# A normalised input transposed by channel tile, with the gain applied on the way out of PSUM

## The chip, the cores and the metric

The kernel runs on one core of one Trainium2 chip. The metric is the device time of one execution in microseconds (us), as the median of several runs. TensorE is called PE in the profile, its weight loads PEld, VectorE DVE, ScalarE ACT, GpSimd POOL and SyncE SP (it issues the DMAs here). Each engine works through its own instructions in order and waits on semaphores for the others.

## The reference, cut to what matters

One layer with two parallel groups of heads (differential attention and a gated recurrence) and a feed-forward block with a convolution. 16 meta tokens stand ahead of 1024 tokens of width 1024. The part concerned is the first normalisation and the first projection:

```python
def rmsnorm(x, g):
    xf = x.astype(jnp.float32)
    y = xf * lax.rsqrt(jnp.mean(xf * xf, axis=-1, keepdims=True) + EPS)
    return (y * g.astype(jnp.float32)).astype(x.dtype)

h = jnp.concatenate([meta, x], axis=1)      # 1040 x 1024
a = rmsnorm(h, ln_mix_pre[l])
proj = a @ w_in[l]                          # 1024 x 3584
```

Attention, the recurrence, the output projection and the feed-forward block follow; the change doesn't touch them.

## The kernel before, in words

Tokens are cut into nine blocks: block 0 has the 16 meta tokens, blocks 1 to 8 have 128 tokens each. Three blocks make a token group, of 272, 384 and 384 tokens (`GROUPS`). The 1024 channels are cut into eight channel tiles of 128.

The projection needs the normalised input with channels on the partitions. It is kept in two parts: `ahi`, the value rounded to the matmul's format, and `alo`, what the rounding left (each 8 tiles by 1040 tokens). Weights are split in the same way into `hi` and `lo`. A product of one channel tile is three matmuls (hi by ahi, hi by alo, lo by ahi; `proj_step`, L218), so one projection of 128 columns for one token group is 24 matmuls into one PSUM bank. They are called products below. Head 0 of the attention is projected first: queries (`dq`), keys (`dk`) and values (`dv`), each for three token groups: 3 x 3 x 24 = 216 products. After it comes head 0's recurrence input (`hf`, the first dense projection), with attention beside it.

Before the change, a block is made ready like this. `pre_stat` (L244): ScalarE squares the block with an accumulator for the row sums, then a logarithm and an exponential give the reciprocal root (`rstd_of`, L157). `pre_scale` (L252): VectorE multiplies block, root and gain in two passes of 512 columns; the gain `gb` lies on all 128 partitions, made at the start by a matmul of a row of ones with the gain row (L793 to L797). `pre_turn` (L257): TensorE transposes four channel tiles of the block into one PSUM bank. `pre_hi` and `pre_lo` (L265, L268): ScalarE copies the bank to `ahi`, VectorE subtracts that from the bank into `alo`, 512 columns each.

The order of TensorE's instructions is that of the program (`manual_schedule`). On the other engines a scheduler orders the instructions, except while `state["ordered"]` is set: then VectorE and ScalarE keep program order, too. `interleave` (L59) decides where side work stands between products: it takes products worth `lead` ns first, then alternately one step of the side work and products worth `fill` ns. Blocks 0 to 2 are made ready by a sequence written out by hand (L789 to L827); `head0_first` (L829) gives the 48 query and key products and the 24 value products of the first token group; blocks 3 to 5 stand among its value products, one half block at a time (L887), and blocks 6 to 8 among head 0's products of the second group (L890). Small constants (`smalls`) and the tables of the relative bias (`bias_tables`, four matmuls) follow. The loads are all on SP's queue: gain, blocks 0 to 2, weights, blocks 3 to 8, then small constants and the next weights.

`pools`: PSUM has three kinds of tiles of two buffers each: `ip` (one bank, for products), `m` (one bank) and `S` (two banks). VectorE's subtraction for the weights' `lo` part stands on GpSimd (`split`, L144; L871 for the value weights).

Of the kernel before, what the change touches and what calls it, by code (L numbers as in the profile page):

```python
# [17 lines left out]
P = 128  # L18
META = 16
# [17 lines left out]
def start(i):  # L37
    return 0 if i == 0 else META + P * (i - 1)
# [20 lines left out]
def interleave(dense, sides, fill, lead=0):  # L59
    sides = list(sides)  # L60
    live = True

    def feed(budget):
        nonlocal live
        while live and budget > 0:
            c = next(dense, False)
            if c is False:
                live = False
            elif c is None:
                return  # L70
# [11 lines left out]
    feed(1e12)  # L82


@with_exitstack
def layer_kernel(ctx: ExitStack, tc: tile.TileContext, x, meta, table, lbl, gpre, gpost, win,
# [54 lines left out]
    def ps_s(name):  # L141
        return pp.tile([P, 2, 512], F32, tag="S", name=name)
# [88 lines left out]
    gb = zp.tile([P, D], F32, tag="gb", name="gb", bufs=1)  # L231
    ones = zp.tile([P, 384], F32, tag="rb", name="ones", bufs=1)[:1, :P]
    G.memset(ones, 1.0)

    xts, xss = {}, {}
# [8 lines left out]
    def pre_stat(i):  # L244
        r = rows(i)
        xss[i] = zp.tile([P, D], F32, tag="xs", name=f"xs{i}", bufs=3)
        ss = zp.tile([P, 1], F32, tag="ss", name=f"ss{i}", bufs=3)
        A.activation(xss[i][:r], xts[i][:r], AF.Square, accum_out=ss[:r])
        rstd_of(ss[:r], ss[:r], D)
        return ss  # L250

    def pre_scale(i, half, ss):  # L252
        r = rows(i)
        cs = slice(512 * half, 512 * half + 512)
        V.scalar_tensor_tensor(xss[i][:r, cs], xts[i][:r, cs], ss[:r], gb[:r, cs], ALU.mult, ALU.mult)

    def pre_turn(i, half, pt):  # L257
        r = rows(i)
        for j in range(4):
            k = 4 * half + j  # L260
            T.transpose(pt[:, j * r:(j + 1) * r], xss[i][:r, P * k: P * (k + 1)], ident[:r, :r])
        pv = pt[:, : 4 * r].rearrange("p (k t) -> p k t", k=4)
        return pv, slice(4 * half, 4 * half + 4), slice(start(i), start(i) + r)

    def pre_hi(pv, ks, s):  # L265
        return A.copy(ahi[:, ks, s], pv)

    def pre_lo(pv, ks, s):  # L268
        return V.tensor_tensor(alo[:, ks, s], pv, ahi[:, ks, s].bitcast(F32), op=ALU.subtract)

    def pre_block(i):
        with tc.issue_after(last_hi.ins):
            ss = pre_stat(i)
        for half in range(2):
            pre_scale(i, half, ss)
        pt = ps_s(f"px{i}")
        for half in range(2):
            out_ = pre_turn(i, half, pt[:, half])
            pre_hi(*out_)
            pre_lo(*out_)  # L280
            yield
# [473 lines left out]
    grow = zp.tile([P, D], F32, tag="xt", name="grow", bufs=3)[:1]  # L755
    SY.dma_start(grow, gpre)
# [4 lines left out]

    def raw_tile(j, c):
        if 2 * j + c < 3 or (j, c) == (1, 0):
            return wp.tile([P, 512], F32, tag="wr", name=f"wr_{tiles[j][1]}_{c}", bufs=3)
        n = 2 * j + c - 3
        return spare[0][:, 512 * n: 512 * (n + 1)]

    raws, parts = {}, [[None, None] for _ in range(3)]

    def load_raw(j, c):  # L770
        raws[j, c] = raw_tile(j, c)
        SY.dma_start(raws[j, c], win[tiles[j][0]][:, 512 * c: 512 * (c + 1)])
# [8 lines left out]
    load_x(5, spare[2][:, D:2 * D])  # L781

    def weights(j, c):
        hi = wp.tile([P, 512], F32R, tag="wh", name=f"wh_{tiles[j][1]}_{c}", bufs=4)
        lo = wp.tile([P, 512], F32R, tag="wl", name=f"wl_{tiles[j][1]}_{c}", bufs=4)
        split(hi, lo, raws[j, c])
        parts[j][c] = hi, lo

    state["ordered"] = True  # L789
    stat = {}  # L790
    for i in range(3):
        stat[i] = pre_stat(i)
    for half in range(2):  # L793
        cs = slice(512 * half, 512 * half + 512)
        pt = ps_m(f"pg{half}")
        T.matmul(pt, ones, grow[:, cs], start=True, stop=True)
        V.tensor_copy(gb[:, cs], pt)  # L797
        if half == 0:
            pre_scale(0, 0, stat[0])
    load_x(6)  # L800
    banks0 = {0: [ps_m(f"px0_{half}") for half in range(2)]}
    for i in (1, 2):
        both = ps_s(f"px{i}")
        banks0[i] = [both[:, half] for half in range(2)]
    turned = {}

    def turn(i, half):
        turned[i, half] = pre_turn(i, half, banks0[i][half])

    for i in (1, 2):  # L810
        for half in range(2):
            pre_scale(i, half, stat[i])
    pre_scale(0, 1, stat[0])
    for i, half in ((0, 0), (1, 0), (1, 1), (2, 0), (2, 1)):
        turn(i, half)
    pre_hi(*turned[0, 0])
    pre_hi(*turned[1, 0])
    weights(0, 0)
    pre_hi(*turned[2, 0])
    for i in range(3):  # L820
        pre_lo(*turned[i, 0])
    weights(1, 0)
    pre_hi(*turned[1, 1])
    weights(0, 1)
    last_hi = pre_hi(*turned[2, 1])
    weights(1, 1)
    load_x(7)  # L827

    def head0_first():  # L829
# [15 lines left out]
        yield from part(0, 0, 1, ahi)  # L845
        yield from part(0, 0, 0, alo)
        yield from part(1, 0, 0, alo)
        yield from part(1, 0, 1, ahi)
# [10 lines left out]
    first_group = head0_first()  # L859
    for _ in range(6):  # L860
        next(first_group)
    turn(0, 1)
    pre_hi(*turned[0, 1])
    for i in range(3):
        last_lo = pre_lo(*turned[i, 1])
    state["ordered"] = False
    third = [ap_.tile([P, 4, 512], F32R, tag="pb", name=f"w3{c}", bufs=2) for c in range(2)]
    for c in range(2):
        with tc.issue_after(last_lo.ins):
            V.tensor_copy(third[c][:, 0], raws[2, c])  # L870
            G.tensor_tensor(third[c][:, 1], raws[2, c], third[c][:, 0].bitcast(F32), op=ALU.subtract)  # L871
        parts[2][c] = third[c][:, 0], third[c][:, 1]

# [7 lines left out]
    def pre_blocks(bs):  # L881
        for i in bs:
            yield from pre_block(i)
            if i == 3:
                load_x(8)

    interleave(first_group, [pre_blocks([3, 4, 5])], 450, 4900)  # L887
    with tc.issue_after(last_lo.ins):
        smalls()
    interleave(head0(1), [pre_blocks([6, 7, 8])], 1800, 1800)  # L890
    interleave(head0(2), [bias_tables()], 2600)
# [630 lines left out]
def _arrays(inputs):  # L1522
    import numpy as np

    def c(a):
        return np.ascontiguousarray(a)
# [10 lines left out]
    for lv in range(5):  # L1537
# [8 lines left out]
        "gpre": c(i["ln_mix_pre"]),  # L1546
# [34 lines left out]
```

## Time and profile before

| what | us |
|---|---|
| median of 3 runs | 1350.29 |
| lowest and highest run | 1346.78, 1351.36 |
| the profiled execution's own time | 1337.81 |
| its span, first to last instruction | 1335.9 |

All durations are from the one profiled execution. In a row of the timeline stand start, duration, engine, line, operation, output<-input, shape and count; in brackets the idle time of the engine before it, and what ended it. In a row of groups stand busy time and the mean duration of one in ns, then the idle time before the group. In a row of windows stand the stretch, then busy time and count of PE, PEld, DVE, ACT and POOL, the granted clock of TensorE as a share of full speed, the DMA engines' share and GB/s. L53 is the helper through which all instructions of VectorE and ScalarE are issued; tiles tell them apart: `xs` the scaled block, `px` a transposed one in PSUM, `pi_dq`, `pi_dk` and `pi_dv` products in PSUM, `ss` sums and roots, `w` the value weights.

### The profile page before, as it was taken

Reading aid. Unit: us, or ns where it says so; the run is one execution under the profiler, and the core shown is the slowest. Engines: PE = TensorE matmul, PEld = TensorE weight load, DVE = VectorE, ACT = ScalarE, POOL = GpSimd, SP = SyncE. Lnnn points to the kernel's source line nnn. Section 1 sums busy time; section 2 is a strip of 40 time slices with the busy share of each in tenths; the row PEclk is TensorE's granted clock in tenths of the full one; section 3 lists DMA queues with packets and bytes.
Section 4 is the critical chain, followed back from the end, with each engine's and each line's share of the span. In section 5 each row is a group of like instructions: output and inputs, shape, how many; then the busy total and the mean of one; then the engine's idle time right before and its main releaser. Section 6 shows DMA issues by size and latency. Waiting matters only on the chain.

```text
span 1335.9 us, 26155 instructions
## 1 busy us (share of the span) xinstructions
PE 1288.3 (96%) x10172; PEld 1187.0 (89%) x10172; DVE 909.4 (68%) x1534; ACT 692.6 (52%) x1633; POOL 426.3 (32%) x334
## 2 busy tenths in 40 slices
PE   7999999999999998999999999999999999999997
PEld 6899989989999998677889999999999998888875
DVE  7565647574746474637798777787787776697586
ACT  7465356535654665237674454444445444454453
POOL 3211212021212110325035666656666640010121
PEclk8999999999999999999999999999999999999999
DMA  5242334143311223657512222223222226955263
GB/s 208 101 141 72 116 119 144 62 140 126 120 48 53 80 88 123 199 182 261 196 48 88 88 91 76 72 92 107 77 90 72 73 95 197 335 185 166 87 205 118
DMA packets 99426, 165.00 MB, mean 124 GB/s; under 512 B 10035, under 2 KB 34899, under 8 KB 99302
## 3 DMA queue, kind: packets, MB, share of 16 engines
q1 hardware_dynamic: 99302, 163.32, 37.2%
q8 instruction: 80, 1.31, 0.4%
q14 instruction: 44, 0.36, 0.1%
HBM read 122.65 MB, written 40.63 MB: 122 GB/s over the span
## 4 chain that ended last, share of the span: by engine, by line
PE 47%; DVE 5%; ACT 3%; issue 3%; DMA 2%; POOL 2%; SPq 0%; DVEq 0%; POOLq 0%; ACTq 0%
PE pd L1427 5%; PE pd L1428 5%; PE pd L1426 5%; PE pb L1268 4%; PE pb L1270 4%; PE pb L1269 4%; PE pc L1268 2%; PE pc L1269 2%; PE pa L1268 2%; PE pa L1270 2%; PE pc L1270 2%; PE pa L1269 2%; PE py L948 1%; PE py L944 1%; PE py L946 1%
## 5 line engine op out<-in xcount | busy, mean ns | idle before, releaser
L1268 PE MATMUL pb<-t,uh 128*128 128x258 f32 x504 | 142.8, 283 | 4.5 <-DVE u L53 4.5
L1269 PE MATMUL pb<-t,uh 128*128 128x258 f32 x504 | 141.7, 281 | 0.0
L1270 PE MATMUL pb<-t,ul 128*128 128x258 f32 x504 | 141.6, 281 | 0.0
L1427 PE MATMUL pd<-wl,gh 128*128 128x512 f32 x308 | 121.9, 396 | 0.1
L1426 PE MATMUL pd<-wh,gh 128*128 128x512 f32 x308 | 121.7, 395 | 0.0
L1428 PE MATMUL pd<-wh,gl 128*128 128x512 f32 x308 | 121.7, 395 | 0.0
L53 DVE SCALAR_TENSOR_TENSOR c<-uu,cwt,c 128x514 f32<-128x514 f32 (+1 forms) x88 | 95.9, 1090 | 20.6 <-ACT c L53 19.9
L1235 POOL TENSOR_TENSOR c<-c,c 128x514 f32<-128x514 f32 (+1 forms) x44 | 63.4, 1440 | 124.7 <-ACT c L53 122.7
L1268 PEld LDWEIGHTS pb<-t,uh 128*128 128x128 f32 x504 | 95.4, 189 | 5.9 <-DVE u L53 5.5
L1269 PEld LDWEIGHTS pb<-t,uh 128*128 128x128 f32 x504 | 95.5, 189 | 0.0
L1270 PEld LDWEIGHTS pb<-t,ul 128*128 128x128 f32 x504 | 95.2, 189 | 0.0
L1268 PE MATMUL pa<-t,uh 128*128 128x258 f32 (+1 forms) x336 | 95.2, 283 | 0.0
L1270 PE MATMUL pa<-t,ul 128*128 128x258 f32 (+1 forms) x336 | 95.0, 283 | 0.0
L1269 PE MATMUL pa<-t,uh 128*128 128x258 f32 (+1 forms) x336 | 94.8, 282 | 0.0
L1268 PE MATMUL pc<-t,uh 128*128 128x258 f32 (+1 forms) x336 | 94.4, 281 | 0.0
L1269 PE MATMUL pc<-t,uh 128*128 128x258 f32 (+1 forms) x336 | 94.0, 280 | 0.0
L1270 PE MATMUL pc<-t,ul 128*128 128x258 f32 (+1 forms) x336 | 93.7, 279 | 0.0
L53 DVE SCALAR_TENSOR_TENSOR c<-ug,cwt,c 128x514 f32<-128x514 f32 (+1 forms) x88 | 84.6, 962 | 2.7 <-ACT c L53 2.0
L147 POOL TENSOR_TENSOR ul<-ws,uh 128x512 fp32r<-128x512 f32 x42 | 60.7, 1445 | 39.4 <-ACT uh L53 34.1
L1427 PEld LDWEIGHTS pd<-wl,gh 128*128 128x128 f32 x308 | 57.7, 187 | 14.9 <-DVE wl L53 0.9
L1426 PEld LDWEIGHTS pd<-wh,gh 128*128 128x128 f32 x308 | 57.7, 187 | 14.1
L1428 PEld LDWEIGHTS pd<-wh,gl 128*128 128x128 f32 x308 | 57.7, 187 | 14.1
(364 smaller groups left out, 4122.0 us busy)
## 6 DMA issues: line engine op xcount, KB each, us to landing
ra<-in_wup_dram SPq DMA_DIRECT2D x88, 256.0 KB, 2.9
mp<-msc SPq DMA_DIRECT2D x23, 512.0 KB, 5.8
wd<-in_wdown_dram SPq DMA_DIRECT2D x44, 256.0 KB, 4.6
tsc<-wd SPq DMA_DIRECT2D x44, 256.0 KB, 3.1
wi<-tsc SPq DMA_DIRECT2D x44, 256.0 KB, 2.8
gi<-gsc SPq DMA_DIRECT2D x33, 256.0 KB, 4.0
wi<-in_wdown_dram SPq DMA_DIRECT2D x33, 256.0 KB, 2.8
gsc<-c SPq DMA_DIRECT2D x22, 257.0 KB, 2.1
```

The costliest lines, as they stand in the source:

```text
L53: ins = call(*args, **kw)
L147: (eng or G).tensor_tensor(lo, raw, hi.bitcast(F32), op=ALU.subtract)
L944: T.matmul(py[:r], mh, hi, start=(first and k == ks[0]), stop=False)
L946: T.matmul(py[:r], mh, lo, start=False, stop=False)
L948: T.matmul(py[:r], ml, hi, start=False, stop=(last and k == ks[-1]))
L1235: G.tensor_tensor(cg, cg, cu, op=ALU.mult)
L1268: T.matmul(pt, hi[:, s], th[:, k], start=(first and k == 0), stop=False, skip_group_check=True)
L1269: T.matmul(pt, hi[:, s], tl[:, k], start=False, stop=False, skip_group_check=True)
L1270: T.matmul(pt, lo[:, s], th[:, k], start=False, stop=(k == 3), skip_group_check=True)
L1426: T.matmul(py, gh[:, s], wh, start=(k == 0 and pr not in (3, 7)), stop=False, skip_group_check=True)
L1427: T.matmul(py, gh[:, s], wl, start=False, stop=False, skip_group_check=True)
L1428: T.matmul(py, gl[:, s], wh, start=False, stop=(k == NH - 1), skip_group_check=True)
```

## The change

Gain, scaling, transposes and copies are arranged by channel tile over the three blocks of a group, instead of by block.

- The gain arrives as a column per channel tile (`gt`, 128 x 8). It is applied when a transposed tile leaves PSUM: ScalarE multiplies by the tile's column into `ahi`, VectorE multiplies and subtracts into `alo` in one instruction. The matmul and the copies that spread the gain go.
- Scaling multiplies a block by its root alone, in place.
- For each channel tile, the transposes of the group's three blocks go side by side into one PSUM bank; one copy and one subtraction of 272 or 384 columns follow. Products can start on a channel tile when that tile is out.
- Squares of blocks 2 (half) and 3 move to VectorE. Roots of blocks 3 to 5 and of 6 to 8 are taken together, after the last square of each three.
- 40 dummy transposes of the identity stand among the first ones.
- The whole of head 0 is one stream of products (`chain_all`), and one stream of side work runs beside it: group 1's tiles, small constants, group 2's tiles, the bias tables. Blocks 7 and 8 are loaded behind the others into the buffers of blocks 0 and 1.

The core of the diff:

```diff
-    def pre_stat(i):
-        A.activation(xss[i][:r], xts[i][:r], AF.Square, accum_out=ss[:r])
-        rstd_of(ss[:r], ss[:r], D)
-    def pre_scale(i, half, ss):
-        V.scalar_tensor_tensor(xss[i][:r, cs], xts[i][:r, cs], ss[:r], gb[:r, cs], ALU.mult, ALU.mult)
...
+    def sq_a(i, cols=slice(0, D)):
+        r = rows(i)
+        return A.activation(junk_a[:r, cols], xts[i][:r, cols], AF.Square, accum_out=ssq[:r, i:i + 1])
+
+    def sq_v(i, cols=slice(0, D), to=None):
+        r, to = rows(i), i if to is None else to
+        return V.scalar_tensor_tensor(junk_v[:r, cols], xts[i][:r, cols], 1.0, xts[i][:r, cols],
+                                      ALU.mult, ALU.mult, accum_out=ssq[:r, to:to + 1])
+
+    def scale(i, cols=slice(0, D)):
+        r = rows(i)
+        V.tensor_scalar(xts[i][:r, cols], xts[i][:r, cols], ssq[:r, i:i + 1], None, ALU.mult)
+
+    def turn(i, k, pt, t0):
+        r = rows(i)
+        o = start(i) - t0
+        T.transpose(pt[:, o:o + r], xts[i][:r, P * k: P * (k + 1)], ident[:r, :r])
+
+    def halves_in(k, pt, t0, t1):
+        s = slice(t0, t1)
+        hi = A.mul(ahi[:, k, s], pt[:, : t1 - t0], gt[:, k:k + 1])
+        return hi, V.scalar_tensor_tensor(alo[:, k, s], pt[:, : t1 - t0], gt[:, k:k + 1], ahi[:, k, s].bitcast(F32), ALU.mult, ALU.subtract)
...
+    def pre_group(g):
+        b0, b1 = GROUPS[g]
+        t0, t1 = start(b0), start(b1 - 1) + P
+        if g > 1:
+            with tc.issue_after(last_hl[0].ins):
+                for i in range(b0, b1):
+                    sq_a(i)
+            rstd_of(ssq[:, b0:b1], ssq[:, b0:b1], D)
+        for i in range(b0, b1):
+            scale(i)
+        banks = px_banks(g)
+        for k in range(KD):
+            pt = next(banks)
+            for i in range(b0, b1):
+                turn(i, k, pt, t0)
+            last_hl[:] = halves_in(k, pt, t0, t1)
+            yield 1 if g < 2 else 2.4
...
+    sq_a(0)
+    rstd_of(ssq[:META, 0:1], ssq[:META, 0:1], D)
+    sq_a(1)
+    rstd_of(ssq[:, 1:2], ssq[:, 1:2], D)
+    sq_a(2, slice(0, 512))
+    scale(0)
+    sq_v(2, slice(512, D), NBLK)
+    V.tensor_tensor(ssq[:, 2:3], ssq[:, 2:3], ssq[:, NBLK:NBLK + 1], op=ALU.add)
+    scale(1)
+    weights(0, 0, V.tensor_copy)
+    rstd_of(ssq[:, 2:3], ssq[:, 2:3], D)
+    for half in range(2):
+        scale(2, slice(512 * half, 512 * half + 512))
+    idle_turns(24)
...
+    for k in range(KD):
+        if k > 3:
+            pxs.append(next(banks0))
+            for i in range(2):
+                turn(i, k, pxs[k], t0)
+        turn(2, k, pxs[k], t0)
+        halves_in(k, pxs[k], t0, t1)
+        if k == 0:
+            weights(1, 0, V.tensor_copy)
+        if k == 3:
+            weights(0, 1, A.copy)
+        if k == 5:
+            weights(1, 1, A.copy)
+        advance((0, 1, 1, 6, 4, 4, 4, 4)[k])
+    for c in range(2):
+        weights(2, c, V.tensor_copy)
+    sq_v(3)
+    sq_a(4)
+    sq_a(5)
+    rstd_of(ssq[:, 3:6], ssq[:, 3:6], D)
+    state["ordered"] = False
+    load_x(7)
+    load_x(8)
+
+    def sides():
+        yield from pre_group(1)
...
+        yield from pre_group(2)
...
-    interleave(first_group, [pre_blocks([3, 4, 5])], 450, 4900)
-    interleave(head0(1), [pre_blocks([6, 7, 8])], 1800, 1800)
-    interleave(head0(2), [bias_tables()], 2600)
+    interleave(chain_all(first_group, head0(1), head0(2)), [sides()], 460, 2300)
```

More of the change, by code (lines that the diff above doesn't have):

```diff
@@ L82, in interleave, with chain_all @@
     feed(1e12)
+def chain_all(*its):
+    for it in its:
+        yield from it
 @with_exitstack
@@ L258, in pre_turn @@
+    def turn(i, k, pt, t0):
         r = rows(i)
[L259 to L269, printed above, removed]
@@ new lines, in px_banks @@
+    def px_banks(g):
+        b = []
+        for k in (0, 2):
+            both = ps_s(f"px{g}_{k}")
+            b += [both[:, 0], both[:, 1]]
+        yield from b
+        yield ps_m(f"px{g}_4")
+        yield ps_m(f"px{g}_5")
+        both = ps_s(f"px{g}_6")
+        yield both[:, 0]
+        yield both[:, 1]
+    last_hl = []
+    def pre_group(g):
[15 more added lines that the diff above has]
+            yield 1 if g < 2 else 2.4
@@ L781, in layer_kernel, with weights @@
     load_x(5, spare[2][:, D:2 * D])
[L783 to L786, printed above, removed]
-        parts[j][c] = hi, lo
[L789 to L827, printed above, removed]
+    load_x(6)
+    def weights(j, c, copy):
+        if j < 2:
+            hi = wp.tile([P, 512], F32R, tag="wh", name=f"wh_{tiles[j][1]}_{c}", bufs=4)
+            lo = wp.tile([P, 512], F32R, tag="wl", name=f"wl_{tiles[j][1]}_{c}", bufs=4)
+        else:
+            both = ap_.tile([P, 4, 512], F32R, tag="pb", name=f"w3{c}", bufs=2)
+            hi, lo = both[:, 0], both[:, 1]
+        copy(hi, raws[j, c])
+        G.tensor_tensor(lo, raws[j, c], hi.bitcast(F32), op=ALU.subtract)
+        parts[j][c] = hi, lo
     def head0_first():
@@ L857, in head0_first @@
             yield from proj_step(pts[2], parts[2], k, t0, t1, lambda: tiles[2][2](0, *g0, t0, t1, pts[2]))
[L859 to L872, printed above, removed]
     def head0(g):
@@ new lines, in layer_kernel, with idle_turns @@
+    pxs = [next(banks0) for _ in range(4)]
+    warm = ps_m("warm")
+    def idle_turns(n):
+        for _ in range(n):
+            T.transpose(warm[:, :P], ident, ident)
+    state["ordered"] = True
+    sq_a(0)
[8 more added lines that the diff above has]
+    weights(0, 0, V.tensor_copy)
```

74 lines of the change are left out of this document (37 added, 37 removed).

## The prediction

> **What bounds the kernel now.** I read the page first: the busy shares, and the row of the granted clock in 40 slices of 33.4 us.
>
> ```profile
> PE 1288.3 (96%) x10172; PEld 1187.0 (89%) x10172; DVE 909.4 (68%) x1534; ACT 692.6 (52%) x1633; POOL 426.3 (32%) x334
> PEclk8999999999999999999999999999999999999999
> ```
>
> TensorE is busy for 96% of the span, so time that TensorE loses early is not won back later. Only the first slice shows a lower clock, and the change lies there. So next come the windows of 10 us, with the granted clock behind the busy times.
>
> ```profile
> 10.00:20.00 10.00, 9.32 (x69) 8.61 (x67) 7.13 (x12) 8.78 (x21) 8.17 (x6) 1.00 0.99 370
> 20.00:30.00 10.00, 5.92 (x27) 5.50 (x27) 8.96 (x19) 6.01 (x16) 0.00 (x0) 0.61 0.25 80
> 30.00:40.00 10.00, 9.51 (x59) 9.08 (x59) 7.79 (x22) 6.79 (x18) 0.00 (x0) 0.88 0.01 2
> 40.00:50.00 10.00, 10.00 (x61) 9.15 (x60) 4.30 (x8) 4.65 (x9) 0.00 (x0) 1.00 0.01 2
> ```
>
> The stretch from 20 to 32 us is what can be won: TensorE is busy for 5.92 of 10 us, at a clock of 0.61. The timeline shows both losses.
>
> ```profile
> 12.17 0.77 PE L837 MATMUL pi_dq<-ahi,wh_dq 128*128 128x272 f32 x4 [0.68 <-ACT ahi L53]
> ...
> 19.69 0.29 PE L222 MATMUL pi_dv<-ahi,w 128*128 128x272 f32 x1
> ...
> 19.81 0.29 PE L224 MATMUL pi_dv<-alo,w 128*128 128x272 f32 x1
> ...
> 23.38 1.11 PE L261 MATMUL px<-ident,xs 128*128 128x128 f32 x4 [3.28 <-DVE alo L53]
> ...
> 26.28 0.43 PE L224 MATMUL pi_dv<-alo,w 128*128 128x272 f32 x1
> 26.51 0.43 PE L226 MATMUL pi_dv<-ahi,w 128*128 128x272 f32 x1
> ...
> 27.96 1.12 PE L261 MATMUL px<-ident,xs 128*128 128x128 f32 x4 [0.80 <-DVE alo L53]
> ...
> 32.94 0.29 PE L224 MATMUL pi_dv<-alo,w 128*128 128x272 f32 x1
> 33.06 0.29 PE L226 MATMUL pi_dv<-ahi,w 128*128 128x272 f32 x1
> ...
> 33.19 0.34 PE L222 MATMUL pi_dq<-ahi,wh_dq 128*128 128x384 f32 x1
> 33.37 0.34 PE L224 MATMUL pi_dq<-alo,wh_dq 128*128 128x384 f32 x1
> ...
> 65.65 0.34 PE L226 MATMUL pi_dv<-ahi,w 128*128 128x384 f32 x1
> ```
>
> Products of 272 columns start 0.12 us apart at 19.7 us. After an idle stretch of 3.28 us they start 0.23 us apart (26.28 to 26.51), and 0.12 apart again at 32.94: the half clock held from 23.4 to about 32.2, that is 8.9 us, with two more gaps in it; from the end of the 0.80 us gap at 27.96 to the return it was 4.3 us. The second token group's products begin at 33.19 (call that point T), and head 0 ends at 66.0.
>
> **The change part by part.** Everything after head 0 keeps its instructions, so I ask when T comes and what lies between T and the end of head 0.
>
> *Start, to the first group's products.* The row matmul of the gain (two 128x512 outputs), two copies of it and the gain in the scaling go; the gain is a per-partition scalar in the instructions that leave PSUM. Block 2's square is shared by two engines. What stays is a chain: squares of blocks 1 and 2, the root, scaling, transposes, copies.
>
> ```profile
> 5.27 1.06 ACT L53 ACTIVATE xs<-xt 128x1024 f32<-128x1024 f32 x1 [0.35 <-DMA xt<-in_x_dram]
> 8.38 0.20 ACT L53 ACTIVATE ss<-ss 128x1 f32<-128x1 f32 x1
> L53 ACT ACTIVATE xs<-X_in 128x1024 f32<-128x1024 f32 x4 | 4.2, 1057 | 0.0
> L53 ACT ACTIVATION_READ_ACCUMULATOR xs<-X_in 128x1 f32 x4 | 0.8, 193 | 0.0
> L53 ACT ACTIVATE ss<-ss,eps 128x1 f32<-128x1 f32 x8 | 2.4, 296 | 0.1
> L53 DVE TENSOR_SCALAR rb<-rb 128x256 f32<-128x256 f32 x4 | 1.5, 366 | 0.1
> L53 DVE TENSOR_SCALAR kr<-kr 128x272 f32<-128x272 f32 x4 | 1.2, 294 | 0.0
> L53 DVE CAST w<-X_in 128x512 fp32r<-128x512 f32 x2 | 1.0, 538 | 0.0
> L53 ACT ACTIVATE kr<-pi_hf 128x272 f32<-128x272 f32 x4 | 1.6, 398 | 1.0 <-PE pi_hf L226 1.0
> ```
>
> Block 2's root ends at 8.6 as before: half a square fewer on ScalarE (0.5 us), but a VectorE addition and a wait for it instead. A scaling reads one tensor and one scalar per partition. The shapes nearest to it take 0.37 us for 256 and 0.29 us for 272 columns. At that slope plus a fixed 0.2, 1024 columns cost 0.75 us and 512 0.48. Without that rate it would be 1.28 us (the row further down). I take 0.75, since both rows are of its form. VectorE does block 1's scaling, one weight cast, then block 2's first half: done at 9.6, and the first copy out of PSUM at 10.05. Each copy covers 272 columns (0.40 us on ScalarE). From channel tile 4 on, TensorE puts four products (0.5 us) between two tiles' transposes and the copies follow it, two weight casts of 0.62 us between them: about 15.9 for the eighth. By the order written in the code, 44 of the 48 query and key products then end by 18.4. Before, 48 of them and 5 value products had run by 19.9. So the start is no faster: the forty dummy transposes only fill time in which TensorE waits anyhow.
>
> *First wait: blocks 3 to 5.* Behind the 44 products stand the transposes of all three blocks. VectorE does two weight casts (to 17.2), then block 3's square of 1024 columns while GpSimd subtracts the same two weight tiles.
>
> ```profile
> 16.87 3.12 POOL L871 TENSOR_TENSOR w<-X_in,w 128x512 fp32r<-128x512 f32 x2 [0.36 <-DVE w L53]
> ...
> 17.31 3.23 DVE L53 SCALAR_TENSOR_TENSOR xs<-X_in,ss,gb 128x512 f32<-128x512 f32 x2 [0.18 <-ACT ss L53]
> ...
> L53 DVE SCALAR_TENSOR_TENSOR a<-xh,ssy,gfb 128x1024 f32<-128x1024 f32 x8 | 10.2, 1281 | 7.8 <-ACT ssy L53 7.7
> L53 DVE SCALAR_TENSOR_TENSOR q<-pi_dq,q 64x272 fp32r<-64x272 f32 x2 | 0.9, 439 | 0.1
> ```
>
> Beside the same two subtractions, two passes of 512 columns took 3.23 us. Elsewhere a pass of 1024 took 1.28. So the square costs between 1.28 and 3.2 us; I take 2.8 (at 17.2 the first subtraction is some way on): 20.0. Root 0.6, scaling 0.75, a query pass of 0.44 that stands between, two scalings: 23.4. (With 1.28 it would be 21.9.) TensorE stands from 18.4 to 23.4, against 3.28 us before; I take it that the clock falls as it did there.
>
> [...]
>
> *From there to T.* Left are 28 products (0.125 us each, 3.5), 24 transposes, and one wait for a PSUM bank at channel tile 5 (a copy and a subtraction, about 0.7).
>
> ```profile
> 40.51 0.34 PE L226 MATMUL pi_dk<-ahi,wl_dk 128*128 128x384 f32 x1
> ...
> 40.68 0.60 PE L261 MATMUL px<-ident,xs 128*128 128x128 f32 x4
> ...
> 41.03 0.42 PE L222 MATMUL pi_dk<-ahi,wh_dk 128*128 128x384 f32 x1
> ```
>
> Four transposes push the next product by 0.35 us (40.68 to 41.03), so 24 cost 2.1. The sum is 6.3 us at full clock. Half clock for 4.3 us adds 2.15 (between 0, if it doesn't fall, and 4.45, if it lasts 8.9). I take 4.3 because the new order has no gap as long as 0.8 us here. T = 23.4 + 6.3 + 2.15 = 31.9, against 33.2: **1.3 us won**.
>
> *Second wait: blocks 6 to 8, new.* Before, each block's square stood early on ScalarE and its transposes in fours behind it. Now the scheduler writes ScalarE's order thus (the built program, as output<-input and size):
>
> ```
> ahi<-px_6_401,gt 128x384          last copy of group 1
> junk_a,ssq<-xt_149 128x1024       square of block 6
> junk_a,ssq<-xt_305 128x1024       square of block 7
> lg<-lg 128x8                      small exponential
> avn_125<-pn_va_0_445 16x128, 128x256   values of group 0
> junk_a,ssq<-xt_307 128x1024       square of block 8
> le<-le 128x2                      small exponential
> ssq<-ssq,eps 128x3 ; ssq<-ssq 128x3    root of all three
> ```
>
> The copies of the values wait for transposes that TensorE does nine products after T. Only then does VectorE scale three blocks, and TensorE's transposes of all three stand only 12 products and three transposes behind T.
>
> ```profile
> 35.40 0.50 ACT L53 COPY avn<-pn_va 16x128 f32<-16x128 f32 x2
> L53 ACT ACTIVATE hq<-pi_hq 128x384 f32<-128x384 f32 x8 | 3.9, 491 | 0.8 <-PE pi_hq L226 0.8
> ```
>
> From T on: the last transposes 0.3, the last copy 0.5, squares of 6 and 7 at 1.2 each with their accumulator reads, 0.2, the value copies 0.5, square of 8 1.2, 0.2, root 0.6, three scalings 2.25, and three handovers of some 0.1 to 0.2: 8.4 us. TensorE is there after 12 products of 0.174 (33.19 to 33.37) and 0.26: 2.35 us. **It waits 6.05 us**, where before nothing waited. No cover is left: every product behind is in TensorE's program order. The idle time is twice that before 23.38, so the clock falls again; 4.3 us at half cost 2.15 more. If TensorE is still slow at T, it comes later to a wait that ends at the same time.
>
> *Rest.* The four bias-table matmuls move by a few products. The loads of blocks 7 and 8 stand behind the small constants on SP; they are needed 2 us after T, over 10 us after they can start. I put both at nothing; a load missing would add to the second wait directly.
>
> Sum: -1.3 + 6.05 + 2.15 = +6.9, say **+7 us** on the profiled execution's 1337.8 us (span 1335.9). That execution lies 12.5 us under the median of the runs, 1350.3; the head of the kernel should differ alike in both, so I forecast 1357.3.
>
> **The rivals.**
> 1. *The clock stays up.* The waits stand, at full clock: T = 29.7, -3.5 + 6.05 = +2.6: 1352.9; with one of the two drops, 4.7 more than before: 1355.0. For it: one observed drop is little evidence. Against it: 3.28 us sufficed there, and both waits are longer. [...]
> 2. *The half clock holds 8.9 us each time*, as it did: T = 34.2, +1.0 + 6.05 + 4.45 = +11.5: 1361.8. Against it: the two gaps that lie in that stretch.
> 3. *Faster: no first wait.* If the square of block 3 and the scalings get through so that blocks 3 to 5 stand ready at 18.4, T = 18.4 + 6.3 = 24.7, and with the second wait and no drop -8.5 + 6.05 = -2.4: 1347.9. It decides at T = 27.1, that is blocks 3 to 5 ready by 20.8. My lower bound is 21.9. For it: 24 products start at 10.5 instead of 12.17.
> 4. *The dummy transposes don't hold the clock.* Then the first group's work is slower, and TensorE reaches the first wait some 2 us later, which ends when VectorE does: +0.
>
> **How the numbers follow.** Forecast 0.55, with its variant 4 in it; rival 1 0.22; rival 2 0.14; rival 3 0.09. A difference of 0.3% (4 us) is about what a measurement tells from none. Slower by more: nearly all of the forecast, rival 2 and part of rival 1, 0.73. Within: most of rival 1 and half of rival 3, 0.21. Faster by more: 0.06, from rival 3 with a shorter second wait. The range takes in rival 2 and most of rival 1: 1352 to 1362.5.
>
> **What would show it.** TensorE idle for about 5 us near 18 to 23, ended by VectorE's scaling; T near 32; a second idle stretch of about 6 us ended by the scalings of blocks 6 to 8, with ScalarE's square of 8 behind the value copies; a granted clock under 1 behind each. I am wrong if the second stretch is under 3 us, if T lies under 27, or if head 0 ends before 66.

## The result, and the profile after

The changed kernel takes 1363.76 us (median of four runs, 1359.67 to 1366.38); the kernel before takes 1348.92 us in the four runs that stand against it. The ratio is 1.0107, with a 95% interval of 1.0074 to 1.0139: **14.8 us slower**. The forecast was 1357.3 with a range of 1352.0 to 1362.5. The direction was right, the size about half of what came, and the time lies outside the range.

The page of the profile after (own time 1363.16 us, span 1361.3) shows TensorE as busy as before. Beside the first slice only the sixth has a lower clock (170 to 204 us, behind the part that changed). The page doesn't tell where the two kernels differ:

```profile
PE 1302.7 (96%) x10208; PEld 1198.5 (88%) x10208; DVE 907.7 (67%) x1537; ACT 692.1 (51%) x1627; POOL 428.9 (32%) x333
PEclk8999989999999999999999999999999999999999
```

The windows of the same stretches as in the prediction do (PE, PEld, DVE, ACT and POOL, then the granted clock, DMA share, GB/s):

```profile
10.00:20.00 10.00, 7.54 (x33) 5.80 (x32) 3.86 (x8) 3.82 (x8) 3.38 (x4) 0.71 0.87 312
20.00:30.00 10.00, 5.97 (x37) 4.93 (x37) 7.24 (x11) 4.36 (x11) 4.40 (x3) 0.84 0.39 137
30.00:40.00 10.00, 7.98 (x46) 6.90 (x45) 4.80 (x9) 5.82 (x12) 0.00 (x0) 0.77 0.00 0
40.00:50.00 10.00, 5.50 (x27) 4.77 (x28) 5.90 (x22) 5.50 (x15) 0.00 (x0) 0.91 0.00 2
```

Before, one of these four windows was bad (20 to 30 us), and the start of the next. Now all four are. From 10 to 20 us TensorE runs 33 matmuls instead of 69, at a clock of 0.71 instead of 1.00: the prediction expected no loss in that window. The waits of TensorE, summed over the span (us in total, times, longest), name the causes. Of the kernel after:

```profile
PE px L266 <- DVE alo L53: 4.4, 7, 1.1
...
PE px L266 <- DVE xt L53: 4.0, 3, 3.4
PE px L266 <- DVE X_in L53: 3.8, 3, 2.8
```

and of the kernel before:

```profile
PE px L261 <- DVE alo L53: 4.6, 3, 3.3
```

`X_in` is the first wait of the prediction, `xt` its second. But seven waits of transposes for `alo`, the subtraction, stand there as well, as much time as before, in small pieces. The timeline shows where they come from (at 31.27 and 35.05 stand two more, of 0.42 us each, at 21.23 one of 0.21):

```profile
10.99 0.50 DVE L53 SCALAR_TENSOR_TENSOR alo<-px,gt,ahi 128x272 fp32r<-128x272 f32 x1 [0.37 <-ACT ahi L53]
11.55 0.33 PE L266 MATMUL px<-ident,X_in 128*128 128x128 f32 x1 [1.11 <-DVE alo L53]
...
13.40 0.33 PE L266 MATMUL px<-ident,X_in 128*128 128x128 f32 x1 [0.56 <-DVE alo L53]
...
14.69 1.11 PE L821 MATMUL pi_dk<-ahi,wh_dk 128*128 128x272 f32 x4
...
21.87 0.49 ACT L53 ACTIVATE ahi<-px,gt 128x272 fp32r<-128x272 f32 x1 [1.23 <-PE px L266]
...
23.47 2.32 DVE L53 SCALAR_TENSOR_TENSOR junk_v<-X_in 128x1024 f32<-128x1024 f32 x1
...
24.19 0.66 PE L821 MATMUL pi_dk<-alo,wh_dk 128*128 128x272 f32 x4
...
27.64 0.33 PE L266 MATMUL px<-ident,X_in 128*128 128x128 f32 x1 [2.79 <-DVE X_in L53]
...
29.60 1.25 PE L821 MATMUL pi_dk<-ahi,wl_dk 128*128 128x272 f32 x4
...
37.08 0.62 DVE L53 SCALAR_TENSOR_TENSOR alo<-px,gt,ahi 128x384 fp32r<-128x384 f32 x1 [0.22 <-ACT ahi L53]
37.76 0.55 PE L266 MATMUL px<-ident,X_in 128*128 128x128 f32 x3 [0.82 <-DVE alo L53]
...
40.46 0.55 PE L266 MATMUL px<-ident,X_in 128*128 128x128 f32 x3 [0.82 <-DVE alo L53]
...
40.76 0.43 PE L227 MATMUL pi_dq<-ahi,wh_dq 128*128 128x384 f32 x1
```

The transpose at 11.55 is that of channel tile 1. It has a bank of its own in PSUM, which no engine has read yet, and still it waits until VectorE has subtracted channel tile 0 (10.99 + 0.50). `px_banks` hands out both banks of one `S` tile (`ps_s`, 128 x 2 x 512) for tiles 0 and 1, and again for 2 and 3 and for the last two. Here a write into the second half waits for the reader of the first, 1.11 us at 11.55. The row at 13.40 is tile 3 behind tile 2, the one at 21.23 tile 7 behind tile 6; those at 31.27, 35.05 and 40.46 are tiles 1, 3 and 7 of blocks 3 to 5. These six waits are 3.5 of the 4.4 us. The seventh, at 37.76, is another thing: tiles 4 and 5 take single banks of kind `m`, the first group's value products hold one of the two (`pi_dv0_0`), so tile 5 waits until tile 4's bank is read (37.08 + 0.62). That is the wait for a bank at tile 5 that the prediction had, at 0.7 us. After the first such gaps the clock falls: four products at 14.69 take 1.11 us, where at 24.19 four take 0.66. The eighth copy starts at 21.87 instead of the forecast's 15.9, the 44 products end at 24.85 instead of 18.4, and T is 40.76.

The second wait is there as described, with the square of block 8 behind the value copies, then the root and three scalings:

```profile
44.25 1.05 ACT L53 ACTIVATE junk_a<-xt 128x1024 f32<-128x1024 f32 x1
...
46.00 2.08 DVE L53 TENSOR_SCALAR xt<-xt,ssq 128x1024 f32<-128x1024 f32 x3
46.81 0.33 PE L266 MATMUL px<-ident,xt 128*128 128x128 f32 x1 [3.37 <-DVE xt L53]
...
48.13 0.39 PE L266 MATMUL px<-ident,xt 128*128 128x128 f32 x1 [0.33 <-DVE xt L53]
...
48.64 0.52 PE L229 MATMUL pi_dq<-alo,wh_dq 128*128 128x384 f32 x1
48.96 0.52 PE L231 MATMUL pi_dq<-ahi,wl_dq 128*128 128x384 f32 x1
...
81.92 0.39 PE L227 MATMUL pi_hf<-ahi,wh_hf 128*128 128x272 f32 x1 [1.36 <-ACT k L53]
```

The last row is the recurrence's first product; I call its start H. H is 81.92 here and 67.30 in the profile of before: 14.6 us, of which 7.6 lie ahead of T (40.76 against 33.19) and 7.05 between T and H (41.16 against 34.11).

### The profile page after: what moved, and what is told of

Same layout as the page of the kernel before. It is cut to its first block, busy times and chain, and to the rows that moved or that the text cites. A ratio compares the mean times of both kernels' runs of the same rounds, so it can differ in the third digit from the quotient of the medians.

```text
span 1361.3 us, 26216 instructions
## 1 busy us (share of the span) xinstructions
PE 1302.7 (96%) x10208; PEld 1198.5 (88%) x10208; DVE 907.7 (67%) x1537; ACT 692.1 (51%) x1627; POOL 428.9 (32%) x333
## 4 chain that ended last, share of the span: by engine, by line
PE 46%; DVE 6%; DMA 3%; issue 3%; POOL 2%; ACT 2%; SPq 0%; DVEq 0%; POOLq 0%; ACTq 0%
PE pd L1462 4%; PE pd L1461 4%; PE pd L1463 4%; PE pb L1303 4%; PE pb L1305 4%; PE pb L1304 4%; PE pc L1303 2%; PE pc L1304 2%; PE pa L1303 2%; PE pa L1305 2%; PE pc L1305 2%; PE pa L1304 2%; PE py L983 1%; PE py L979 1%; PE py L981 1%
## 5 line engine op out<-in xcount | busy, mean ns | idle before, releaser
L1461 PEld LDWEIGHTS pd<-wh,gh 128*128 128x128 f32 x308 | 57.7, 187 | 14.1
L1463 PEld LDWEIGHTS pd<-wh,gl 128*128 128x128 f32 x308 | 57.7, 187 | 14.1
```

What stands on the lines that cost most here:

```text
L1461: T.matmul(py, gh[:, s], wh, start=(k == 0 and pr not in (3, 7)), stop=False, skip_group_check=True)
L1463: T.matmul(py, gl[:, s], wh, start=False, stop=(k == NH - 1), skip_group_check=True)
```

## The experiments

My theory after the result (**P**): the two banks of an `S` tile count as one object for waits; its odd tiles' waits and the half clock behind them make what the forecast lacks, and the rest is what the forecast had. The rival: the arrangement by channel tile is slow by itself in the first 25 us (copies, thin TensorE, clock), whatever the banks. Ratios are to the kernel before, run on the same chip, with 95% intervals.

**e0: the kernel before, unchanged.** The profile of before was taken from an execution 11 us under its own runs' median, so a second one was needed to read T and H against.

> The kernel before, unchanged, for a second profile. Its first profile was 1337.8 us, 11 us under the median of its runs, so 10.8 us of the 25.4 us between the two profiles are left after head 0 (there it is 14.6 us). Theory (the later difference is the granted clock's phase, not the change): a time near 1349, the second token group's first product at 33 us and the first recurrence product at 67 us as in the first profile, and granted clock under 1 in stages after 100 us that the first profile doesn't show. Rival (the change itself costs 10 us later on): a profile of 1338 again, with a clock of 1.00 after 67 us.

Ratio 1.0013 (0.9995 to 1.003): no difference. Its second profile:

```profile
23.27 0.66 PE L261 MATMUL px<-ident,xs 128*128 128x128 f32 x4 [3.27 <-DVE alo L53]
...
32.19 0.34 PE L222 MATMUL pi_dq<-ahi,wh_dq 128*128 128x384 f32 x1
...
66.37 0.39 PE L222 MATMUL pi_hf<-ahi,wh_hf 128*128 128x272 f32 x1 [1.34 <-ACT k L53]
```

T and H are 1.0 and 0.9 us earlier than in the first profile, though the span is 6.9 us longer (1342.8). So what makes these two executions of one kernel differ lies behind H (the granted clock from 180 to 201 us, for one, is 0.92 here, 1.00 there). H is therefore compared in what follows, with the mean of the two, 66.8, for before.

**e1: the same pairs, handed out to tiles that aren't neighbours.**

```diff
-        for k in (0, 2):
-            both = ps_s(f"px{g}_{k}")
-            b += [both[:, 0], both[:, 1]]
-        yield from b
+        b = [ps_s(f"px{g}_0"), ps_s(f"px{g}_1")]
+        yield b[0][:, 0]
+        yield b[1][:, 0]
+        yield b[0][:, 1]
+        yield b[1][:, 1]
         yield ps_m(f"px{g}_4")
-        yield ps_m(f"px{g}_5")
-        both = ps_s(f"px{g}_6")
-        yield both[:, 0]
-        yield both[:, 1]
+        b = ps_s(f"px{g}_5"), ps_s(f"px{g}_6")
+        yield b[0][:, 0]
+        yield b[1][:, 0]
+        yield ps_m(f"px{g}_7")
```

> The changed kernel, with neighbouring channel tiles in different PSUM tiles: the order of banks is first half of one pair, first half of the other, second halves, then a single bank, two pairs' first halves, a single bank. Theory P (an odd channel tile's transposes wait for the even tile's subtraction because both banks of a pair are one tile, and these gaps also let the clock fall in the first group): the waits of TensorE on VectorE's alo, 4.4 us in all, are nearly gone; the 44 products of the first group end at 18 to 20 us instead of 24.9; T (first product of the second group) at 32 to 34 instead of 40.8; the time 7 to 9 us under the changed kernel, about 1355 to 1357. Rival C (the clock falls anyway, since TensorE is thinly occupied while it waits for copies): only the 4.4 us of gaps go at best, T at 37 to 39, 2 to 4 us won, about 1360.

1355.43 us, ratio 1.0056 (1.0034 to 1.0077). The timeline of this kernel:

```profile
18.15 0.49 ACT L53 ACTIVATE ahi<-px,gt 128x272 fp32r<-128x272 f32 x1 [0.55 <-PE px L266]
...
23.89 0.30 PE L266 MATMUL px<-ident,X_in 128*128 128x128 f32 x1 [2.78 <-DVE X_in L53]
...
25.86 1.25 PE L821 MATMUL pi_dk<-ahi,wl_dk 128*128 128x272 f32 x4
...
33.00 0.43 PE L227 MATMUL pi_dq<-ahi,wh_dq 128*128 128x384 f32 x1
...
39.14 1.05 PE L266 MATMUL px<-ident,xt 128*128 128x128 f32 x2 [3.46 <-DVE xt L53]
...
74.34 0.39 PE L227 MATMUL pi_hf<-ahi,wh_hf 128*128 128x272 f32 x1 [1.28 <-ACT k L53]
```

Of the `alo` gaps one of 0.29 us is left (at 12.68), the clock from 10 to 20 us is 1.00, and H is 7.6 us earlier than in the kernel after. Nothing but the hand-out of banks differs, so the hand-out is the cause, and its price is about half of the loss. It took the bank wait at tile 5 (0.82 us) away as well, since tile 5 now lies in an `S` tile; the pairs' own share may be smaller by that. The two ratios (1.0107 and 1.0056) differ by 0.5%, some 7 us; they were not run side by side, and their intervals just touch. e2 and e4 below differ in the hand-out, too (and in how three scalings are spread): 1.0093 against 1.0037, with intervals that lie apart. The rival isn't empty: the 44 products end at 21.1 us, where theory P had 18 to 20, and before had 48 and five value products done by 20.1. What is left, +7.5 us, is near the forecast's +7: T stands with before (33.00 against 33.19 and 32.19), and T to H is 41.3 us against 34.1. The second wait and the half clock behind it are what this kernel loses.

**e2: the squares of blocks 6 to 8 early, pairs as in the kernel after.** Squares behind the copies of tiles 2, 3 and 4 of group 1; root and three scalings behind tile 5.

```diff
...
+            if g == 1 and k in (2, 3, 4):
+                with tc.issue_after(last_hl[0].ins):
+                    sq_a(k + 4)
+            if g == 1 and k == 5:
+                with tc.issue_after(last_hl[0].ins):
+                    rstd_of(ssq[:, 6:9], ssq[:, 6:9], D)
+                for i in range(6, 9):
+                    scale(i)
```

> The changed kernel, with the squares of blocks 6 to 8 on ScalarE behind the copies of channel tiles 2, 3 and 4 of group 1, root and scaling behind tile 5. Theory S (the wait behind T is ScalarE's order, worth its 5 us plus 1.6 us of half clock behind it): the wait of 5 us at T + 2.7 is gone and the clock stays up behind T; T itself moves up to 2 us later, since the scalings stand ahead of tile 6's subtraction, on which tile 7 waits; in all 4 to 6 us under the changed kernel, about 1358 to 1360. Rival (the wait is taken up by a later one anyway, for the recurrence's first product at 81.9 us waits for key copies): the wait goes, but that product comes at 81 to 82 us all the same and the time is within 1 us of the changed kernel.

1358.84 us, ratio 1.0093 (1.0067 to 1.0119). A miss: H is only 1.8 us earlier than in the kernel after, and by the ratios 1.9 us are won, where 4 to 6 us were expected. (The time itself lies in the expected 1358 to 1360, but before is 3 us faster on this chip, too.)

```profile
43.03 0.55 PE L266 MATMUL px<-ident,X_in 128*128 128x128 f32 x3 [2.49 <-DVE alo L53]
...
80.12 0.39 PE L227 MATMUL pi_hf<-ahi,wh_hf 128*128 128x272 f32 x1 [1.38 <-ACT k L53]
```

The second wait is gone (T to H is 36.8 us instead of 41.2), but T is 2.6 us later: the scalings now stand on VectorE ahead of tile 6's subtraction, and tile 7, the other half of the same pair, waits 2.49 us for that. The work that was moved off one wait landed in the next one of the same engine.

**e3: dummy transposes to hold the clock.** Ten of the identity before tiles 1 to 4 of group 0, forty before each long wait.

```diff
+        fill = ps_m(f"fill{g}")
+        for _ in range(40 if g == 1 else 40):
+            T.transpose(fill[:, :P], ident, ident)
...
+        if 0 < k < 5:
+            idle_turns(10)
```

> The changed kernel with more dummy transposes and nothing else: 10 ahead of the transposes of each of the channel tiles 1 to 4 of the first group, 40 ahead of blocks 3 to 5, 40 ahead of blocks 6 to 8. Rival C (the clock is the cause): at full clock they take about 0.06 to 0.09 us each, so they fit into the waits or cost under 1 us where they don't; the products of the first group start 0.12 us apart instead of 0.23, the 44 end 3 to 4 us earlier, the clock is up behind both long waits (1.6 us behind the second, about 3 behind the first): 6 to 8 us won, about 1357. Theory P (the waits are the cause, the clock a follower): the odd tiles' waits stay; T moves by 2 to 4 us, and 3 to 5 us are won in all, about 1359 to 1361.

1361.76 us, ratio 1.0101 (1.0077 to 1.0124). The windows of this kernel:

```profile
20.00:30.00 10.00, 9.35 (x79) 8.87 (x78) 7.42 (x12) 4.62 (x12) 4.91 (x3) 1.00 0.47 163
30.00:40.00 10.00, 6.49 (x49) 5.62 (x48) 5.02 (x9) 5.59 (x12) 0.00 (x0) 1.00 0.01 2
40.00:50.00 10.00, 9.79 (x74) 9.16 (x73) 5.50 (x21) 6.01 (x15) 0.00 (x0) 1.00 0.01 2
```

The clock is at 1.00 all through, T is 39.81 and H 79.62: 2.3 us earlier than in the kernel after, of which 1.35 lie behind T. That is less than either side expected (6 to 8 us, 3 to 5 us). With a full clock TensorE only comes sooner to the next wait for VectorE: in group 1 the three pairs' waits and the one at tile 5 are 0.82 to 1.04 us each. From the first wait on, the waits are the cause and the clock follows. In group 0 the dummies cost time themselves (ten take 1.26 us; the 44 products end at 24.89, as in the kernel after), so for that part this kernel gives no clean price of the clock.

**e4: e1 and e2 together**, with one scaling behind each of the subtractions of tiles 5, 6 and 7 instead of three in a row.

```diff
...
+            if g == 1 and k >= 5:
+                with tc.issue_after(last_hl[1].ins):
+                    scale(k + 1)
```

> The changed kernel with both findings undone: neighbouring channel tiles in different PSUM tiles (as in e1_alternate), and the squares of blocks 6 to 8 behind the copies of tiles 2 to 4 of group 1, the root behind tile 5, one scaling behind each subtraction from tile 5 on. Theory (the whole loss is these two, and they add): T at 33 to 34 us as in e1_alternate, the wait behind T under 1 us, the recurrence's first product at 66 to 68 us as in the kernel before, and the time within 0.15% of the kernel before. Rival (something else of the change costs, such as the clock, which also fell at the wait for blocks 3 to 5, or the tables' new places): that product at 70 us or later, and the time 3 to 5 us above the kernel before.

1350.96 us, ratio 1.0037 (1.0017 to 1.0057). Most of both losses is gone (H 71.47, 10.4 us earlier than in the kernel after), but before, which I had expected to reach within 0.15%, isn't reached: it is the rival's numbers that came (H at 70 us or later, 3 to 5 us above before).

```profile
24.99 0.45 PE L266 MATMUL px<-ident,X_in 128*128 128x128 f32 x1 [2.79 <-DVE X_in L53]
...
39.95 0.33 PE L266 MATMUL px<-ident,xt 128*128 128x128 f32 x1 [0.86 <-DVE sub L53]
...
71.47 0.39 PE L227 MATMUL pi_hf<-ahi,wh_hf 128*128 128x272 f32 x1 [1.28 <-ACT k L53]
```

T to H is 35.9 us, 1.7 more than before; the second wait of 3.46 us has come down to 0.86. The rest stands ahead of T (35.58, where e1 had 33.00). The first wait is as long as in e1 (2.79 us), so it doesn't make the difference. It ends 1.1 us later, for the clock fell in group 0 (0.83 from 10 to 20 us, with e1's instructions on TensorE); half clock behind it takes 0.55 us more. The last 0.9 us, from tile 5's transposes to T (2.84 us against 1.91), looks like the price of the early squares: on ScalarE they stand between the copies of tiles 2 to 5 (1.05 us each, at 30.91, 32.96 and 34.46), and tile 7 waits 0.46 us.

**e6: e4 with the first wait shortened.** The scalings of blocks 3 to 5 go ahead of the value weights' two casts on VectorE.

```diff
-    for c in range(2):
-        weights(2, c, V.tensor_copy)
     sq_v(3)
     sq_a(4)
     sq_a(5)
     rstd_of(ssq[:, 3:6], ssq[:, 3:6], D)
+    for i in range(3, 6):
+        scale(i)
+    for c in range(2):
+        weights(2, c, V.tensor_copy)
```

> e4_alt_early, and in the wait for blocks 3 to 5 the two casts of the value weights moved behind the scalings, so that block 3's square doesn't run beside GpSimd's subtractions. Theory (in that wait VectorE's square is slowed by GpSimd, 2.3 us instead of 1.3, and stands behind 0.8 us of casts): the wait of TensorE for blocks 3 to 5, 4.2 us in e1_alternate, falls by 1.8 to 2.3 us, T comes at 30 to 31.5, and the time is 2 to 4 us under the kernel before. Rival (the wait moves on to the value weights, whose casts and subtractions are now late): T as in e4_alt_early within 0.7 us, with TensorE waiting for the value weights in place of the blocks.

1350.51 us, ratio 1.0031 (1.0013 to 1.0049). A miss again: T was expected at 30 to 31.5 and came at 33.09, and the kernel stays over before.

```profile
23.79 0.30 PE L266 MATMUL px<-ident,X_in 128*128 128x128 f32 x1 [1.41 <-DVE X_in L53]
...
68.83 0.40 PE L227 MATMUL pi_hf<-ahi,wh_hf 128*128 128x272 f32 x1 [1.15 <-ACT k L53]
```

The wait halved, but the value products then waited 0.40 us for GpSimd's `w`, and waits of 0.61, 0.47 and 0.86 us came behind. By this time every wait that the prediction named had been shortened, and the arrangement by channel tile stood no better than the one by block.

**e5: the kernel before, with a PSUM tile of its own for each half block.** If theory P is right, the 3.28 us wait of before is the same thing: the second half of block 3 waits for the first half's subtraction, since both lie in one `S` tile.

```diff
-        pt = ps_s(f"px{i}")
         for half in range(2):
-            out_ = pre_turn(i, half, pt[:, half])
+            out_ = pre_turn(i, half, ps_s(f"px{i}_{half}")[:, 0])
```

> The kernel before, with the two halves of a block's transposes for blocks 3 to 8 in PSUM tiles of their own instead of the two banks of one. Theory P (the rule that cost the changed kernel its 4.4 us of gaps is also what stops the kernel before for 3.3 us at 23.3 us and 0.5 to 2 us after it: the second half's transposes wait for the first half's subtraction): these waits are gone or under 1 us, the clock stays up, T at 27 to 29 us instead of 32 to 33, and the time is 3 to 5 us under the kernel before. Rival (VectorE's work is late there anyhow, its scaling runs beside GpSimd): the wait at 23 us turns into one for the scaled block, T moves by less than 2 us.

1343.56 us, ratio 0.9975 (0.9959 to 0.999): by the ratio 3.4 us faster than before (the medians differ by 2.4), and so **faster than both kernels**, by little.

```profile
23.52 0.66 PE L261 MATMUL px<-ident,xs 128*128 128x128 f32 x4 [0.73 <-DVE alo L53]
25.47 0.63 PE L261 MATMUL px<-ident,xs 128*128 128x128 f32 x4 [0.79 <-DVE xs L53]
28.85 0.63 PE L261 MATMUL px<-ident,xs 128*128 128x128 f32 x4 [0.92 <-DVE lmx L53]
...
29.70 0.34 PE L222 MATMUL pi_dq<-ahi,wh_dq 128*128 128x384 f32 x1
...
64.70 0.39 PE L222 MATMUL pi_hf<-ahi,wh_hf 128*128 128x272 f32 x1 [1.78 <-ACT k L53]
```

Waits under 1 us stand in place of 3.27, 2.02 and 0.58; the clock from 20 to 40 us is 1.00, where e0 had 0.91 and 0.92. T came at 29.70, a little behind the expected 27 to 29: this execution started slower, four products taking 1.28 us at 12.35 where the first profile of before has 0.77 at 12.17, and its 48 products ended 1.7 us later (20.77 against 19.03). Against this version e6, which is rid of most of its neighbours' waits too, is 0.56% behind (1.0031 against 0.9975, both run on one chip).

**e7: e1 without the forty dummy transposes** of the start, for the prediction's sentence that they only fill time, against its rival 4.

```diff
-    idle_turns(24)
...
-    idle_turns(8)
...
-    idle_turns(8)
```

> e1_alternate without the 40 dummy transposes at the start. Variant 4 of the prediction (the dummy transposes only fill time in which TensorE waits, and what the first group loses it loses before a wait that ends when VectorE does): T and the time within 1 us of e1_alternate. Rival (they hold the clock up, and all that follows hangs on TensorE's pace, since the copies, the squares and the scalings come after its transposes): the first group's products start 0.23 us apart, its 44 products end 2 to 4 us later, and T and the time are 2 to 4 us above e1_alternate.

1355.7 us, ratio 1.007 (1.0045 to 1.0096), beside e1's 1.0056: not told apart by the time. The timeline:

```profile
10.05 0.87 ACT L53 ACTIVATE ahi<-px,gt 128x272 fp32r<-128x272 f32 x2 [1.52 <-PE px L266]
...
25.45 0.45 PE L266 MATMUL px<-ident,X_in 128*128 128x128 f32 x1 [2.79 <-DVE X_in L53]
...
75.47 0.39 PE L227 MATMUL pi_hf<-ahi,wh_hf 128*128 128x272 f32 x1 [1.27 <-ACT k L53]
```

The first copy starts at 10.05 us, where e1 has 10.86: the last dummies run until block 2's transposes can start at 10.55, so they don't only fill time. But without them four products take 1.25 us at 15.02 (e1 0.75 at 14.77), and the 44 end 1.5 us later (22.66 against 21.11), near the 2 us of rival 4. The first wait is as long as in e1 and its end moves along (25.45 against 23.89), T is 2.3 us later (35.31), where rival 4 had "+0"; at H 1.1 us of it is left. Two single profiles carry this, and the times don't settle it.

**All of them together.** How much later H is than 66.8, beside the ratio in us (of 1346, the kernel before on those chips):

| kernel | H later by | time more, interval |
|---|---|---|
| after | 15.1 | 14.4 (10.0 to 18.7) |
| e2 | 13.3 | 12.5 (9.0 to 16.0) |
| e3 | 12.8 | 13.6 (10.4 to 16.7) |
| e7 | 8.6 | 9.4 (6.1 to 12.9) |
| e1 | 7.5 | 7.5 (4.6 to 10.4) |
| e4 | 4.6 | 5.0 (2.3 to 7.7) |
| e6 | 2.0 | 4.2 (1.7 to 6.6) |
| e5 | -2.1 | -3.4 (-5.5 to -1.3) |

In each row the first number lies within the interval of the second. The intervals are wide, but the table fits a cost that is lost ahead of H and carried to the end; nothing behind H needs a cause of its own.

## Why the prediction was right or wrong

**Where it looked** was right: TensorE is busy for 96% of the span, and what is lost early is lost. The table above bears that out for eight kernels, within its intervals.

**Start, to the first group's products: the step that failed.** The prediction had "TensorE puts four products between two tiles' transposes and the copies follow it", "about 15.9 for the eighth" copy, and the 44 products done "by 18.4". Measured: 21.87 and 24.85, 6.4 us late at the end. I had counted the banks one by one and overlooked that the two of an `S` tile are one object to the waits. e1 divides the miss. With the pairs apart the eighth copy starts at 18.15 and the products end at 21.1 (23.89 - 2.78): 3.7 us of the 6.4 are the pairs together with the half clock, which can come without them (below). Of the other 2.7, 0.8 stands at the first copy, forecast for 10.05: e1 has 10.86, and 10.05 came in e7, without the dummies. The last 1.9 are my cadence: I counted four products of 0.125 us for each tile from the fifth on, and e1 shows a tile every 1.03 us (copies at 15.05, 16.08, 17.12, 18.15), since its three transposes stand there as well (0.35 us, 15.45 to 15.80).

**First wait: the size was right, the place wrong.** Forecast 18.4 to 23.4, measured 24.85 to 29.6, 4.75 us against 5.0. Square, root and scalings all stand on VectorE behind the eighth subtraction, so the wait's end moves with the copies: the first product behind it starts 7.73 us after the eighth copy in the kernel after (29.60 - 21.87) and 7.71 in e1 (25.86 - 18.15). This is also where rival 4 was worked out wrongly. "It ends when VectorE does: +0" takes VectorE for independent; it hangs on TensorE's transposes. The square took 2.32 us beside GpSimd's two subtractions, against 2.8 taken and 1.28 to 3.2 as bounds. The two subtractions started at 23.30 and 24.7 and took 1.41 and 2.28 us, and the square, from 23.47 on, ended between their ends, at 25.79. In e6, with GpSimd idle, the square took 1.22 us, so 1.1 us less; what passes between the two engines isn't shown.

**From there to T.** Forecast 8.45 us, with 2.15 for the half clock and 0.7 for a bank at tile 5; measured 11.2 (29.6 to 40.76). The wait at tile 5 came as forecast (0.82). Three more, at tiles 1, 3 and 7 (0.42, 0.42 and 0.82 us), are the pairs', which the forecast didn't have. The last 0.9 us isn't divided here; the low clock lasted 5.0 us behind 29.6, against 4.3. In e1, without these four waits, it is 7.1 (25.86 to 33.00).

**Second wait: right in kind and place, 1.3 us too long.** It was to end 8.4 us after T and ended 7.4 after it (48.13 against 40.76), by the scalings, with the square of block 8 behind the value copies. TensorE stood 3.37 + 0.34 + 0.33 us, around two single transposes, 4.7 us in all (43.44 to 48.13) against 6.05: the end came 1.0 us earlier after T than worked out, and TensorE was there 0.3 us later. The clock fell again (products 0.32 us apart at 48.64, against 0.17) and came back at 51.7, at a cost of about 1.7 us against 2.15. T to H grew by 7.05 us, forecast 8.2. e1, which keeps this wait and not the pairs', loses 7.5; e2 and e4, which take it away, win 4.4 and 5.5 between T and H (against the kernel after and e1).

**The sum.** -1.3 at T was +7.6, 8.9 us off: 6.4 from the start, 2.7 from the way to T, -0.25 from the first wait. Behind T the forecast was 1.15 us too high. So the term at T makes more than all of the miss. The total of +7 came in a kernel without the pairs, e1, and that was in part luck: there the start is 2.7 us late, and a shorter first wait (4.75 us) and a shorter way to T (7.1 against 8.45) take 1.6 of it back.

**The rivals.** Rival 3 (faster) needed blocks 3 to 5 ready by 20.8; they were ready at 29.5. Rival 1 (the clock stays up) was tried as e3: 2.3 us of 14.8. The prediction valued the two drops at 4.3 us, because it added them to waits that end at a time of their own. Rival 2 (the half clock holds 8.9 us each time) came nearest in us and for the wrong reason: behind the second wait the clock was low for 3.4 us, and the loss was in new waits. Both rivals took the 8.9 us and the wait of 3.28 us from one profile; in e0, with a wait of 3.27 us, the clock didn't fall there at all (last section).

**What stays open.** How much of group 0's loss is the clock's. TensorE has the same instructions there in e6 as in e1, with the same gaps (0.47, 0.29 and 0.35 us); e1 shows 1.00 from 10 to 20 us and e6 0.83 (e4 as well), its eighth copy 1.25 us later. So the fall is no sure consequence of the pairs' gaps, and how the 3.7 us divide between gaps and clock isn't known: by e6 the clock can make a third of them. Which gaps or waits bring the clock down isn't shown. Single profiles scatter by about as much at T, and differences of 1 us between them are no more than hints. Why e6 isn't ahead of before isn't pinned on one wait either.

## What to carry to other kernels

In these kernels two banks taken as one PSUM tile are one object when waits are made (tile 1 waits 1.11 us in the kernel after and not at all in e1; block 3's second half 3.27 us in e0 and 0.73 in e5): count buffers by what is allocated, not by banks, and look in the waits for a transpose that waits on the reader of another tile. Before such a wait is put down to that, see whether a single bank is simply not free yet, as at tile 5 here. When an engine's chain is said to end "by itself", follow it back to its first input; if that is the engine which waits, both move together. Compare a late marker that every execution reaches, like H here, rather than two spans.

## What the runs showed of the hardware

The granted clock, read in windows of 1 us, fell in the kernel after at 14.1 us. TensorE's longest gap between 10 us and there was 1.11 us, with 0.34 and 0.56 behind it, and one product stood there for each copy. In e6 it fell between 13.69 and 14.95, with no gap over 0.47 us from 9 us on:

```profile
13.46 0.39 PE L823 MATMUL pi_dq<-ahi,wh_dq 128*128 128x272 f32 x1 [0.35 <-ACT ahi L53]
13.69 0.78 PE L823 MATMUL pi_dk<-ahi,wh_dk 128*128 128x272 f32 x4
...
14.95 1.25 PE L823 MATMUL pi_dq<-alo,wh_dq 128*128 128x272 f32 x4
```

Four products take 0.78 us at 13.69 and 1.25 us at 14.95.

In the kernel after, the clock fell to 0.50 and came back to 1.00 by turns at 14.14, 20.96, 27.78, 34.62, 48.26 and 51.68 us, each dated by the share of the low clock in its window of 1 us. These times are 6.82, 6.82, 6.84, 13.64 and 3.42 us apart, within 0.02 us of whole multiples of 3.41. By the shares in the windows of 10 us from 10 to 50 us, with the low clock taken as 0.50, it lasted 3.4 us in e0, 3.4 and 6.8 in e1 and e4, 3.4 and 7.0 in e7, and 3.4 in e6. In the first profile of before it lasted 10.2 us, from 22.20 to 32.44. With waits of 3.28 and 3.27 us the first profile of before fell at 22.20, inside the wait, and e0 at about 28.2, only behind its second wait (2.02 us).

In e3, with its added dummies, the clock reads 1.00 in every window to 85 us. In e7 it reads 1.00 from the beginning to 20 us, though four products took 1.25 us at 15.02 and 0.75 at 18.38: the row doesn't show that slow stretch.
